# A trunk of two mixer layers on one core: three stage borders, and the second gate stage moved into the attention's filler

## The chip, the cores and the metric

The kernel runs on one core of one Trainium2 chip. Its time is device microseconds of that core for one execution; three executions were timed, and the median counts. One more execution was profiled, and all rows below are from it.

## The reference

All tensors are float32, 1024 tokens by 1024 channels.

```python
def reference(x, p, norm_pre, norm_post, pe_proj, pe_gate, ...):
    h = x
    for i in range(DEPTH):                       # 2 layers
        u = rmsnorm(h, norm_pre[i])
        if i % 2 == 0:
            y = ab_mixer(u, ...)                 # retention and mLSTM heads, @ w_out
        else:
            y = cd_mixer(u, ...)                 # sparse attention and S5 groups, @ w_out
        h = h + rmsnorm(y.astype(h.dtype), norm_post[i])
        h = h + jax.nn.sigmoid(h @ pe_gate[i]) * (p[i] @ pe_proj[i])
    return h
```

`ab_mixer` projects u to the queries, keys, values and gates of 4 retention and 4 mLSTM heads, and multiplies their gated outputs (1024 + 1024 channels) by `w_out`. `cd_mixer` has 16 query heads in 4 groups that attend to compressed, selected and windowed keys (three softmaxes, weighted by gates), and 32 groups of a state-space model with a gated linear unit; 1024 + 512 channels go to its `w_out`. The line with `sigmoid` is what the text calls the gate stage of a layer.

## The kernel before

Every float32 operand of a product is split into a high and a low part (`hi`, `lo`; `split_tile`, `transpose_split`, `load_w`): ScalarE copies the high part, VectorE or POOL subtracts it for the low part, and a product is three matmuls (high by high, low by high, high by low) into one PSUM bank. A 128x1024 by 1024x512 product is thus 24 matmuls of 512 columns. Tokens lie in 8 row tiles of 128; a tile is transposed by TensorE, four 128x128 blocks to a bank (`trp`), before it can be the stationary operand.

The stages in order are: projections and heads of layer 0, each head's results written to DRAM (`mixR` of the retention, `mixM` of the mLSTM); `out_stage(mixR)`, then `out_stage(mixM)`, whose `sink_m` adds the two, normalises (`post_norm`, L894 to L904) and writes `hD[0]`; the gate stage of layer 0 (`gate_stage`), which also prepares the transposed input of layer 1; the projections of layer 1; the sparse attention; the gate stage of layer 1. `in_pairs` runs `front(i)` (load and transpose tile i) ahead of `proj(i, hf)`, the products of a tile's left and right column half.

The whole program is recorded first; a list scheduler then sets each engine's own order by its model of times and by priorities, and each engine executes its list in order, with semaphores between them. SP's list is a DMA queue of its own: a load that waits holds up all loads behind it. A tile pool gives a buffer again when its last reader is done, so a load into a buffer that is still read waits.

The sparse attention is a loop over 32 units, (group, row tile), 8 for each of 4 groups; `group` loads a group's keys and values, `head` a unit's queries and makes its compressed scores, `scores` and `scale` make the probabilities of window and selection, `values` transposes them (`pt`) and multiplies them by the values (`av`). PSUM has there 1 bank for `cs` and `ct`, 2 for scores, 3 for transposes, 1 for `av`, and 1 (`pF`) for the filler. The filler is a generator of other work, which `step` advances by a credit (`share`, so many steps per group): the S5 gated unit, its output product, `p @ pe_proj` (to `ppD`), the output products of the groups, and for the tiles in `LAST[:-NL]`, which are seven of eight, the last output product, the post-norm and the write of `hD[2]`. The post-norm of such a tile (`s` is ScalarE, `v` VectorE, `g` POOL):

```python
for hf in range(2):
    v.tensor_tensor(y[hf], y[hf], product(T, wq[hf], 2), op=OP.add)
    s.activation(ftile(), y[hf], AF.Square, accum_out=ms[:, hf:hf + 1])
...
    s.activation(y[hf], y[hf], AF.Copy, scale=r)
    g.tensor_tensor(y[hf], y[hf], gp, op=OP.mult)
    g.tensor_tensor(y[hf], y[hf], x, op=OP.add)
```

After the attention, all 8 banks go to layer 1's gate stage (`psA`, 3, and `psB`, 5), which reads `hD[2]` tile by tile, and makes the eighth tile (`late_tile`) along the way.

## Time and profile before

| | us |
| --- | --- |
| median of 3 executions | 2372.84 |
| lowest and highest | 2370.55, 2377.94 |
| the profiled execution | 2377.24 |
| its span, first to last instruction | 2375.2 |
| TensorE busy | 2285.4 |
| VectorE, ScalarE, POOL busy | 1467.8, 1069.0, 488.9 |

The span is shorter than the execution's time by what lies ahead of the first and behind the last instruction. Busy times are sums over all stages; which engine is waited for differs from stage to stage. TensorE's mean granted clock over the span is 0.983 of 2.4 GHz.

### The profile page before, as it was taken

Reading aid. Unit: us, or ns where it says so; the run is one execution under the profiler, and the core shown is the slowest. Engines: PE = TensorE matmul, PEld = TensorE weight load, DVE = VectorE, ACT = ScalarE, POOL = GpSimd, SP = SyncE. Lnnn points to the kernel's source line nnn. Section 1 sums busy time; section 2 is a strip of 40 time slices with the busy share of each in tenths; the row PEclk is TensorE's granted clock in tenths of the full one; section 3 lists DMA queues with packets and bytes.
Section 4 is the critical chain, followed back from the end, with each engine's and each line's share of the span. In section 5 each row is a group of like instructions: output and inputs, shape, how many; then the busy total and the mean of one; then the engine's idle time right before and its main releaser. Section 6 shows DMA issues by size and latency. Waiting matters only on the chain.

```text
span 2375.2 us, 34462 instructions
## 1 busy us (share of the span) xinstructions
PE 2285.4 (96%) x11974; PEld 1910.6 (80%) x11974; DVE 1467.8 (62%) x3877; ACT 1069.0 (45%) x2329; POOL 488.9 (21%) x585
## 2 busy tenths in 40 slices
PE   7999999999999999899999999989999989999898
PEld 6888789788887888788888889878888778777677
DVE  6777647755554435344287352368878888888833
ACT  6233323433332332223232232257877777778821
POOL 0122200000000001100000010034445245566610
PEclk9999999999999999999999999989999999999999
...
GB/s 159 91 80 104 101 45 72 27 73 35 63 54 32 261 142 205 125 71 133 113 193 239 142 76 125 95 155 79 106 171 109 124 133 103 139 137 177 145 158 113
DMA packets 264647, 279.26 MB, mean 118 GB/s; under 512 B 54384, under 2 KB 196312, under 8 KB 264442
## 3 DMA queue, kind: packets, MB, share of 16 engines
...
## 4 chain that ended last, share of the span: by engine, by line
PE 85%; DVE 6%; DMA 5%; issue 2%; ACT 1%; SPq 1%; POOL 0%; ACTq 0%; DVEq 0%; POOLq 0%
PE pj L139 41%; PE gp L139 8%; PE op L139 7%; PE fp L139 5%; PE av L139 4%; PE pt L1448 4%; PE sc L139 4%; PE yp L139 2%; PE gl L139 2%; PE trp L214 2%; DVE pr L1424 1%; DVE pthl L1408 1%; DMA q<-aqD 1%; PE pp L139 1%; PE cs L139 1%
## 5 line engine op out<-in xcount | busy, mean ns | idle before, releaser
L139 PE MATMUL pj<-whi,uh 128*128 128x512 f32 (+2 forms) x768 | 277.4, 362 | 4.2 <-ACT whi L163 2.6
L139 PE MATMUL pj<-wlo,uh 128*128 128x512 f32 (+2 forms) x768 | 277.2, 361 | 0.0
L139 PE MATMUL pj<-whi,ul 128*128 128x512 f32 (+2 forms) x768 | 277.0, 361 | 0.0
L1427 ACT ACTIVATE pr<-pr,nm 128x640 f32<-128x640 f32 (+7 forms) x256 | 187.1, 732 | 65.3 <-DVE nm L1424 58.4
L139 PE MATMUL pj<-vh,whi 128*128 128x512 f32 x512 | 204.0, 399 | 0.2 <-ACT vh L218 0.2
L139 PE MATMUL pj<-vh,wlo 128*128 128x512 f32 x512 | 201.9, 394 | 0.0
L139 PE MATMUL pj<-vl,whi 128*128 128x512 f32 x512 | 200.4, 391 | 0.0
L1408 DVE TENSOR_TENSOR pthl<-pt,pthh 128x512 fp32r<-128x512 f32 x264 | 176.6, 682 | 22.0 <-ACT pthh L1407 20.3
L164 DVE SCALAR_TENSOR_TENSOR wlo<-raw,gnp,whi 128x512 fp32r<-128x512 f32 (+3 forms) x248 | 142.4, 610 | 77.2 <-ACT whi L163 76.3
L139 PE MATMUL gp<-whi,mhl 128*128 128x512 f32 x512 | 167.8, 402 | 6.4 <-DVE mhl L219 4.4
L163 ACT ACTIVATE whi<-raw,gnp 128x512 fp32r<-128x512 f32 (+3 forms) x248 | 134.9, 605 | 77.7 <-PE pj L139 34.6
L1448 PE MATMUL pt<-consts,pr 128*128 128x128 f32 x1056 | 164.3, 280 | 5.1 <-DVE pr L1441 1.7
L139 PEld LDWEIGHTS pj<-whi,uh 128*128 128x128 f32 x768 | 144.9, 189 | 27.3 <-ACT whi L163 2.9
L139 PE MATMUL op<-whi,mhl 128*128 128x512 f32 x520 | 165.4, 396 | 0.6 <-ACT mhl L470 0.6
L139 PEld LDWEIGHTS pj<-wlo,uh 128*128 128x128 f32 x768 | 145.2, 189 | 22.6 <-issue 0.7
L139 PEld LDWEIGHTS pj<-whi,ul 128*128 128x128 f32 x768 | 145.0, 189 | 22.2 <-issue 0.2
L1407 ACT ACTIVATE pthh<-pt 128x512 fp32r<-128x512 f32 x264 | 148.7, 591 | 31.0 <-PE pt L1448 22.8
L139 PE MATMUL sc<-kh,q 128*128 128x320 f32 (+5 forms) x384 | 145.5, 381 | 17.3 <-DVE nm L1424 15.8
L1448 PEld LDWEIGHTS pt<-consts,pr 128*128 128x128 f32 x1056 | 132.2, 144 | 31.7 <-DVE pr L1441 2.4
L1441 POOL TENSOR_SCALAR pr<-pr,cf 128x640 f32<-128x640 f32 (+4 forms) x64 | 114.0, 1782 | 98.5 <-DVE cf L1436 49.5
L139 PE MATMUL sc<-kl,q 82*128 82x320 f32 (+5 forms) x384 | 129.9, 340 | 0.0
L139 PEld LDWEIGHTS gp<-whi,mhl 128*128 128x128 f32 x512 | 97.1, 191 | 29.2 <-DVE mhl L219 5.1
...
## 6 DMA issues: line engine op xcount, KB each, us to landing
...
```

The source lines that it names most:

```text
L139: return t.matmul(o, l, r, start=start, stop=stop, **k)
L163: s.activation(hi[:, k], raw[:, k], AF.Copy, scale=gain(kt0 + k))
L164: v.scalar_tensor_tensor(lo[:, k], raw[:, k], gain(kt0 + k), hi[:, k].bitcast(FT), op0=OP.mult, op1=OP.subtract)
L214: t.transpose(ps[:, k * 128:(k + 1) * 128], x[:, (k4 + k) * 128:(k4 + k + 1) * 128], ident)
L1407: s.activation(hi[:dst_shape], ps[:dst_shape], AF.Copy)
L1408: v.tensor_tensor(lo[:dst_shape], ps[:dst_shape], hi[:dst_shape].bitcast(FT), op=OP.subtract)
L1424: v.tensor_tensor_reduce(pr[:, x:y], ps[:, :y - x], mask[:, x:y], op0=OP.add, op1=OP.min, scale=-1.0, scalar=nm[:, 0:1] if c else 3e38, ac ...
L1427: s.activation(pr[:, :nk], pr[:, :nk], AF.Exp, scale=-1.0, bias=nm[:, c:c + 1], accum_out=sums[:, b, h:h + 1])
L1441: (v if eng == "v" else g).tensor_scalar(P[h][:, :nk], P[h][:, :nk], cf[:, h:h + 1], None, op0=OP.mult)
L1448: t.transpose(ps[:, h * 128:(h + 1) * 128], P[h][:, k * 128:(k + 1) * 128], ident)
```

## The change

Border 1: while the mLSTM's last head is finished, the first three row tiles of `mixR` are loaded on SP's queue into buffers that held queries and keys, and that pool stays open until `out_stage(mixR)` ends. Border 2: `out_stage(mixM)` calls `ahead(i)`, which loads row tile 0 of `hD[0]` after it was written, and transposes and splits it before the stage is over; `gate_stage` takes it from `early`. In `proj` the gate's product is issued ahead of that with `pe_proj`. Border 3: `group` loads all keys, then the values; the probabilities of unit 0 are made inside the projections, between their last blocks. The gate stage of layer 1 becomes part of the filler: for all 8 tiles of `LAST`, the filler makes the output product, post-norm, transposes (`ft`, in the filler's one bank), split, and the gate of the left columns (`gated_out(i, 0, ...)`); the split parts go to DRAM (`gT`). Behind the attention, `rest` reads them back and makes the right halves, with the two banks of the scores, in turn with what is left of the filler. The separate stage is removed. `share` has other numbers, `fhi` and `flo` have two buffers, `ppD` is stored times 0.5.

```diff
+            if h == 3 and i in (2, 3, 4):
+                x = first_rows[i - 2] = p2.tile([128, 1024], FT, name="mt", tag="qkq"[i - 2])
+                nc.sync.dma_start(x, mixR[(i - 2) * 128:(i - 1) * 128, :])
...
+            mt = first_rows.pop(i, None)
+            if mt is None:
+                mt = pm_.tile([128, 1024], FT, name="mt", tag="mt")
+                nc.scalar.dma_start(mt[:, :nkt * 128], src[i * 128:(i + 1) * 128, :nkt * 128])
             return split_tile(pw, mt, nkt)
...
+            X = early.get(i)
+            if X is None:
...
+            ps = psA.tile([128, 512], FT, name="gp", tag="psA")
+            proj_tok(ps, local(*T), i, wq[hf], 512)
...
+    early = {}
+    def ahead(i):
+        if i == 4:
+            early[0] = xh_.tile([128, D], FT, name="h1", tag="h1")
+            nc.sync.dma_start(early[0], hD[0][:128, :])
+        if i == 6:
+            hi, lo = (xl_.tile([128, 2, 512], FR, name=n, tag=n).rearrange("p a (b n) -> p (a b) n", n=128)
+                      for n in ("whi", "wlo"))
+            transpose_split(early[0], 0, hi, lo)
+            early[0] = early[0], (hi, lo)
+    out_stage(pr_, mixM, Wo, 8, Ext(dict(a=xa_, b=xb_, l=xl_, m=xm_), "mmllaabb"), gain, sink_m, after=ahead)
...
+            K[b] = kh, kl
+        for b in (1, 0):
+            vt = wsp.tile([128, 2, 512], FR, name="vt", tag=("whi", "wlo")[b]).rearrange("p a (i d) -> p (a i) d", d=128)
             nc.sync.dma_start(vt.bitcast(FT), vD[:, 4 * b + gg].rearrange("(i p) a d -> p i (a d)", p=128))
-            K[b] = kh, kl, vt
...
+        def probabilities(K, hd, u, b, sums):
+            gg, i = u
+            P = scores(K[b], hd[0], hd[1], i, b, hd[3], sums)
+            scale(P[0], P[2], b, sums, gate_of(gg, i))
+            return P
+        hs_, first = {}, {}
+        for n, _ in enumerate(gen):
+            if n in (2, 7):
+                hs_[len(hs_)] = head(*units[len(hs_)])
+            if n == 10:
+                KV = {0: group(0)}
+            if n in (12, 13):
+                if not first:
+                    sums0 = nh.tile([128, 2, 4], FT, name="sums", tag="sums")
+                first[13 - n] = probabilities(KV[0], hs_[0], units[0], 13 - n, sums0)
...
-            wq = wlast[0] = [[load_w(W2, [(hf * 512, 512)], 6, 2)] for hf in range(2)]
-            for i in LAST[:-NL]:
+            wq = [[load_w(W2, [(hf * 512, 512)], 6, 2)] for hf in range(2)]
+            gw[0] = [load_w(Wg, [(0, 512)], 2 * k, 2, wp=xf) for k in range(4)]
+            gw[1] = [load_w(Wg, [(512, 512)], 0, 2)]
+            for i in LAST:
...
-                    nc.sync.dma_start(hD[2][rows, hv[hf]], y[hf])
+                nc.sync.dma_start(hD[2][rows, hv[1]], y[1])
                 yield
-        wlast = [None]
+                hi, lo = (pf.tile([128, 4, 256], FR, name=n, tag=n, bufs=2).rearrange("p a (b k) -> p (a b) k", k=128)
+                          for n in ("fhi", "flo"))
+                for hf in range(2):
+                    ps = pF.tile([128, 512], FT, name="ft", tag="pf")
+                    for k in range(4):
+                        t.transpose(ps[:, k * 128:(k + 1) * 128], y[hf][:, k * 128:(k + 1) * 128], ident)
+                    p3_, ks = ps.rearrange("p (k n) -> p k n", k=4), slice(4 * hf, 4 * hf + 4)
+                    s.activation(hi[:, ks], p3_, AF.Copy)
+                    v.tensor_tensor(lo[:, ks], p3_, hi[:, ks].bitcast(FT), op=OP.subtract)
+                    yield
+                if i != LAST[-1]:
+                    for a, x in enumerate((hi, lo)):
+                        nc.sync.dma_start(gT[i, :, a, :], x.bitcast(FT).rearrange("p k n -> p (k n)"))
+                yield from gated_out(i, 0, (hi, lo), y[0], pF, "pf")
+                if i == LAST[-1]:
+                    yield from gated_out(i, 1, (hi, lo), y[1], pF, "pf")
+        def gated_out(i, hf, T, h, pool_, tag):
+            rows, hs = slice(i * 128, (i + 1) * 128), slice(hf * 512, (hf + 1) * 512)
+            ps = pool_.tile([128, 512], FT, name="gp", tag=tag)
+            for k in range(0, 8, 4):
+                proj_tok(ps, local(*(x[:, k:k + 4] for x in T)), 0, gw[hf][k // 2:], 512, nkt=4, start=k == 0, stop=k == 4)
+                yield
+            pp = pf.tile([128, 512], FT, name="pp", tag="fin", bufs=4)
+            nc.sync.dma_start(pp, ppD[rows, hs])
+            th = pf.tile([128, 512], FT, name="th", tag="fo", bufs=4)
+            s.activation(th, ps, AF.Tanh, scale=0.5)
+            v.scalar_tensor_tensor(th, th, 1.0, pp, op0=OP.add, op1=OP.mult)
+            (v if done else g).tensor_tensor(th, th, h, op=OP.add)
+            nc.sync.dma_start(dst_[rows, hs], th)
...
+        def rest():
+            def fetch(i):
+                T = [np_.tile([128, 1024], FR, name="g" + x, tag="pr0", bufs=5).rearrange("p (k n) -> p k n", k=8) for x in "hl"]
+                h = np_.tile([128, 640], FT, name="gr", tag="pr1", bufs=4)[:, :512]
+                for a in range(2):
+                    nc.sync.dma_start(T[a].rearrange("p k n -> p (k n)").bitcast(FT), gT[i, :, a, :])
+                nc.sync.dma_start(h, hD[2][i * 128:(i + 1) * 128, 512:])
+                return T, h
+            X = {0: fetch(LAST[0])}
+            for n, i in enumerate(LAST[:-1]):
+                if n + 1 < len(LAST) - 1:
+                    X[n + 1] = fetch(LAST[n + 1])
+                T, h = X.pop(n)
+                yield from gated_out(i, 1, T, h, pS, "sc")
...
-        share = {0: 30, 1: 26, 2: 20, 3: 64}
+        credit = [0.0]
+        share = {0: 24, 1: 34, 2: 22, 3: 50}
...
+        gw[1] += [load_w(Wg, [(512, 512)], 2 * k, 2) for k in range(1, 4)]
+        done.append(True)
+        gens = [fill, fill, rest()]
+        while gens:
+            for x in list(gens):
+                if x in gens and next(x, gens) is gens:
+                    gens = [y for y in gens if y is not x]
...
-    qx_ = ExitStack()
-    psB = qx_.enter_context(tc.tile_pool(name="psB2", bufs=5, space=PSUM, reuse_waits="tile"))
-    psA = qx_.enter_context(tc.tile_pool(name="psA2", bufs=3, space=PSUM, reuse_waits="tile"))
...
-        def late_tile(i, y):
...
-        gate_stage(pw, 1, ext1, hD[2], out if out is not None else dbg["o"], ppD=ppD, order=[7, 6, 5, 0, 1, 2, 4, 3],
-                   late={i: late_tile for i in LAST[-NL:]})
```

The first place is the second border, where the last output matmuls of layer 0 are followed by the first gate products. VectorE's rows of before (`y1` are the output rows under post-norm, `mhl` is the pair of high and low parts, `trp` the bank of the transposes):

```order
L224 TENSOR_SCALAR rsa_9000<-ms_8998 128x1 [waits Activation_49]
L902 SCALAR_TENSOR_TENSOR y1_8940<-y1_8940,rsb_9002,gpost_8317 128x1024 [waits Pool_49]
L903 TENSOR_TENSOR y1_8940<-y1_8940,xr_9004 128x1024 [waits DMAHW2_49,DVE_49]
L1006 TENSOR_TENSOR y1_8968<-y1_8968,op_9009 128x512 [waits PE_49]
L224 TENSOR_SCALAR rsa_9038<-ms_9036 128x1 [waits Activation_49]
L902 SCALAR_TENSOR_TENSOR y1_8968<-y1_8968,rsb_9040,gpost_8317 128x1024 [waits Pool_49]
L903 TENSOR_TENSOR y1_8968<-y1_8968,xr_9042 128x1024 [waits DMAHW5_49,DVE_49]
L219 TENSOR_TENSOR mhl_9112<-trp_9113,mhl_9112 128x512 [waits Activation_49]
L219 TENSOR_TENSOR mhl_9112<-trp_9120,mhl_9112 128x512 [waits Activation_49]
L936 TENSOR_TENSOR pT_9132<-ptp_9129,pT_9132 128x256 [waits DMAHW5_49,Activation_49]
```

and of the change, where tile 0's parts are called `whi` and `wlo`, since they lie in weight buffers:

```order
L1016 TENSOR_TENSOR y1_8942<-y1_8942,op_8973 128x512 [waits PE_49]
L219 TENSOR_TENSOR wlo_9012<-trp_9020,whi_9011 128x512 [waits Activation_49]
L224 TENSOR_SCALAR rsa_9002<-ms_9000 128x1 [waits Activation_49]
L909 SCALAR_TENSOR_TENSOR y1_8942<-y1_8942,rsb_9004,gpost_8317 128x1024 [waits Pool_49]
L910 TENSOR_TENSOR y1_8942<-y1_8942,xr_9006 128x1024 [waits DMAHW1_49,DVE_49]
L1016 TENSOR_TENSOR y1_8970<-y1_8970,op_9027 128x512 [waits PE_49]
L224 TENSOR_SCALAR rsa_9056<-ms_9054 128x1 [waits Activation_49]
L909 SCALAR_TENSOR_TENSOR y1_8970<-y1_8970,rsb_9058,gpost_8317 128x1024 [waits Pool_49]
L910 TENSOR_TENSOR y1_8970<-y1_8970,xr_9060 128x1024 [waits DMAHW4_49,DVE_49]
L945 TENSOR_TENSOR pT_9133<-ptp_9130,pT_9133 128x256 [waits Activation_49]
L219 TENSOR_TENSOR mhl_9138<-trp_9139,mhl_9138 128x512 [waits Activation_49]
L219 TENSOR_TENSOR mhl_9138<-trp_9146,mhl_9138 128x512 [waits Activation_49]
```

Tile 0's second low part (`wlo_9012<-trp_9020`) has moved ahead of the last two post-norms (L909, L910); the low parts of tile 1 (`mhl_9138`) stand where tile 0's stood.

The second place is the border from the projections to the sparse attention. SP's rows of before (`vt` is a group's value tile, `kh` and `kl` its keys, `q2` and `q3` a unit's queries, `zt` a projection's result on its way to DRAM):

```order
L1113 DMA zD_92<-zt_13660 128x512 [waits DMAHW2_49,DVE_49]
L1113 DMA zD_92<-zt_13705 128x512 [waits DMAHW3_49,DVE_49]
L1128 DMA vt_13674<-vD_88 128x8x128 [waits DMAHW4_49,PE_49]
L1126 DMA kl_13673<-kD_87 64x1024 [waits DMAHW5_49,PE_49]
L1127 DMA kl_13673<-akD_89 18x1024 [waits DMAHW6_49]
L1113 DMA zD_92<-zt_13734 128x512 [waits DMAHW7_49,DVE_49]
L1124 DMA kh_14753<-kD_87 64x1024 [waits DMAHW0_49,PE_49]
L1125 DMA kh_14753<-kD_87 64x1024 [waits DMAHW1_49]
```

and of the change:

```order
L1136 DMA zD_92<-zt_13709 128x512 [waits DMAHW4_49,DVE_49]
L1136 DMA zD_92<-zt_13790 128x512 [waits DMAHW5_49,DVE_49]
L1353 DMA q2_14150<-qD_86 128x4x128 [waits DMAHW6_49,PE_49]
L1354 DMA q3_14151<-qD_86 64x4x128 [waits DMAHW7_49,PE_49]
L1355 DMA q3_14151<-aqD_91 18x4x128 [waits DMAHW0_49]
L1153 DMA vt_13653<-vD_88 128x8x128 [waits DMAHW1_49,PE_49]
L1153 DMA vt_13651<-vD_88 128x8x128 [waits DMAHW2_49,PE_49]
L1146 DMA kh_14585<-kD_87 64x1024 [waits DMAHW3_49,PE_49]
L1147 DMA kh_14585<-kD_87 64x1024 [waits DMAHW4_49]
```

All keys of group 0 are loaded earlier; the queries of unit 2 and then both value tiles stand behind the last projection results, and each value tile still waits for TensorE.

The third place is the end of the program. TensorE's rows of before, in the separate gate stage (`h1` is a tile of rows, `gp` the bank of a product):

```order
L139 MATMUL gp_23963<-whi_23490,mhl_23691 128x512 x2
L139 MATMUL gp_23963<-wlo_23491,mhl_23691 128x512
L214 MATMUL trp_23885<-consts_75,h1_23849 128x128 [waits DVE_49,PE_49]
L214 MATMUL trp_23885<-consts_75,h1_23849 128x128 x3
L214 MATMUL trp_23892<-consts_75,h1_23849 128x128 [waits PE_49]
L214 MATMUL trp_23892<-consts_75,h1_23849 128x128 x3
L139 MATMUL gp_23963<-whi_23490,mhl_23691 128x512
L139 MATMUL gp_23995<-whi_23472,mhl_23834 128x512 [waits Activation_49]
L139 MATMUL gp_23995<-wlo_23473,mhl_23834 128x512
L139 MATMUL gp_23995<-whi_23472,mhl_23834 128x512 x2
```

and of the change (`fp` is the bank of an output product, `ft` that of the transposes, `fy` the row halves after the post-norm; tile 1 of the last four):

```order
L139 MATMUL fp_23397<-whi_21652,fhi_23341 128x512 [waits Activation_49]
...
L139 MATMUL fp_23397<-whi_21652,flo_23342 128x512 [waits Pool_49]
...
L139 MATMUL fp_23407<-whi_21658,fhi_23341 128x512 [waits DVE_49]
...
L1613 MATMUL ft_23496<-consts_75,fy_23337 128x128 [waits DVE_49,Pool_49]
L1613 MATMUL ft_23496<-consts_75,fy_23337 128x128 x3
L1613 MATMUL ft_23558<-consts_75,fy_23338 128x128 [waits DVE_49,Pool_49]
L1613 MATMUL ft_23558<-consts_75,fy_23338 128x128 x3
L139 MATMUL gp_23567<-whi_21664,fhi_23494 128x512 [waits DVE_49]
```

Before, the next tile's transposes stand among the products of another; now a tile's output products, transposes and gate products follow one another. The transposes wait for POOL, whose rows for that tile are:

```order
L226 TENSOR_TENSOR rsb_23477<-rsa_23475,mhalf_79 128x1 [waits DVE_49]
L1604 TENSOR_TENSOR fy_23337<-fy_23337,fin_23479 128x512 [waits DMAHW3_49,Activation_49]
L1604 TENSOR_TENSOR fy_23338<-fy_23338,fin_23486 128x512 [waits DMAHW2_49,PE_49,DMAHW5_49,Activation_49,Pool_49]
L1605 TENSOR_TENSOR fy_23337<-fy_23337,fin_23480 128x512 [waits DMAHW4_49,Pool_49]
L1605 TENSOR_TENSOR fy_23338<-fy_23338,fin_23487 128x512 [waits DMAHW6_49,Pool_49]
L1497 TENSOR_TENSOR flo_23629<-zn_22725,fhi_23628 128x2x128 [waits PE_49,Activation_49]
L226 TENSOR_TENSOR rsb_23693<-rsa_23691,mhalf_79 128x1 [waits DVE_49]
```

These are the power of the norm (L226), the two halves times the gain (L1604), the residual added to them (L1605), the low part of the next tile's input (L1497), and the next tile's power.

## Rows read from the trace of the kernel before

**Rows 1.** The page, part 1: busy time, share of the span, instructions.

```profile
PE 2285.4 (96%) x11974; PEld 1910.6 (80%) x11974; DVE 1467.8 (62%) x3877; ACT 1069.0 (45%) x2329; POOL 488.9 (21%) x585
```

**Rows 2.** The page, part 4: the chain that ended last, by engine.

```profile
PE 85%; DVE 6%; DMA 5%; issue 2%; ACT 1%; SPq 1%; POOL 0%; ACTq 0%; DVEq 0%; POOLq 0%
```

**Rows 3.** Windows: stretch, length, busy us (instructions) per engine, clock, DMA share, GB/s.

```profile
960.00:1000.00 40.00, 33.56 (x148) 26.96 (x148) 16.34 (x21) 8.52 (x16) 5.35 (x4) 0.87 0.37 120
...
1545.00:1592.00 47.00, 40.25 (x187) 32.29 (x187) 28.33 (x84) 26.06 (x46) 19.45 (x14) 0.78 0.72 182
...
2035.00:2160.00 125.00, 116.28 (x645) 96.60 (x643) 106.49 (x281) 98.02 (x185) 76.92 (x65) 0.99 0.48 148
...
2160.00:2262.00 102.00, 89.52 (x449) 68.24 (x447) 87.55 (x267) 83.44 (x206) 68.13 (x68) 0.93 0.53 169
```

**Rows 4.** Windows: the half-clock stretches behind the second border and the attention.

```profile
970.40:980.60 10.20, 5.79 (x13) 4.11 (x14) 5.73 (x4) 1.40 (x2) 2.78 (x2) 0.50 0.54 177
...
2264.00:2270.80 6.80, 4.44 (x19) 3.91 (x19) 3.75 (x5) 1.66 (x3) 3.56 (x2) 0.50 0.82 278
```

**Rows 5.** The chain in order of time, last stage: start, us, what.

```profile
2346.07 0.87 PE trp L214 x8
...
2346.95 22.44 PE gp L139 x96
...
2370.77 0.69 DVE h L956
```

**Rows 6.** The same view at the first border.

```profile
769.89 3.60 DMA mt<-mixR
```

**Rows 7.** Timeline at the first border, ScalarE: start, us, engine, line, instruction.

```profile
770.77 1.93 ACT L163 ACTIVATE whi<-raw,cols 128x512 fp32r<-128x512 f32 x3
```

**Rows 8.** Timeline at the second border (idle time before, and its releaser, in brackets).

```profile
966.68 1.23 DVE L903 TENSOR_TENSOR y<-y,xr 128x1024 f32<-128x1024 f32 x1
...
970.42 0.80 PE L139 MATMUL gp<-whi,mhl 128*128 128x512 f32 x1 [2.06 <-ACT mhl L218]
...
971.88 2.41 POOL L160 TENSOR_TENSOR wlo<-raw,whi 128x1024 fp32r<-128x1024 f32 x1 [1.11 <-ACT whi L159]
...
972.12 3.25 DVE L903 TENSOR_TENSOR y<-y,xr 128x1024 f32<-128x1024 f32 x1
...
976.03 1.22 PE L139 MATMUL gp<-whi,mhl 128*128 128x512 f32 x2 [4.38 <-DVE mhl L219]
```

**Rows 9.** The chain in order of time at the third border.

```profile
1545.47 4.77 DMA vt<-vD
...
1550.33 8.80 DMA vt<-vD
...
1559.14 8.38 DMA fin<-y5D
```

**Rows 10.** Groups by line, attention: xcount | busy, mean ns | idle before, releaser.

```profile
L1555 DVE TENSOR_TENSOR fy<-fy,fp 128x512 f32<-128x512 f32 x14 | 9.5, 680 | 3.5 <-issue 2.9 <-PE fp L139 0.4
...
L1556 ACT ACTIVATE fin<-fy 128x512 f32<-128x512 f32 x14 | 8.8, 626 | 5.1 <-DVE fy L1555 4.2 <-issue 0.5 <-POOL fy L1566 0.4
...
L1564 ACT ACTIVATE fy<-fy,rsb 128x512 f32<-128x512 f32 x14 | 9.3, 718 | 1.1 <-POOL rsb L226 1.1
...
L1565 POOL TENSOR_TENSOR fy<-fy,fin 128x512 f32<-128x512 f32 x14 | 17.8, 1286 | 8.0 <-ACT fy L1564 4.9 <-DMA fin<-in_norm_post_dram 2.5 <-ACT pthh L1407 0.6
...
L1566 POOL TENSOR_TENSOR fy<-fy,fin 128x512 f32<-128x512 f32 x14 | 19.0, 1368 | 0.0
```

**Rows 11.** The same view before the attention, POOL: the power of the norms.

```profile
L226 POOL TENSOR_TENSOR rsb<-rsa,mhalf 128x1 f32<-128x1 f32 x24 | 13.4, 559 | 335.2 <-DVE rsa L224 335.2
```

**Rows 12.** Timeline after the attention, TensorE.

```profile
2266.36 1.97 PE L214 MATMUL trp<-consts,h 128*128 128x128 f32 x8 [4.55 <-DMA h<-hD]
```

**Rows 13.** Groups by line, last stage: the two halves of a split.

```profile
L219 DVE TENSOR_TENSOR mhl<-trp,mhl 128x512 fp32r<-128x512 f32 x16 | 10.8, 686 | 10.1 <-ACT mhl L218 9.9
...
L218 ACT ACTIVATE mhl<-trp 128x512 fp32r<-128x512 f32 x16 | 9.0, 596 | 14.4 <-PE trp L214 14.1
```

135 lines of the change are left out of this document (53 added, 82 removed).

## The prediction

> **What bounds the kernel now.** I read the page first: TensorE is busy for 2285 of the 2375 us [rows 1], and the chain that ended last is TensorE for 85% and waits on VectorE and DMA for most of the rest [rows 2]. So an edit is worth what it takes from TensorE's idle time, from its stretches at half clock, or from the last matmul's tail. Next I cut the span into stages [rows 3] to see where TensorE stands still: in the steady stages it is full, and what is lost lies at the borders and in the sparse attention. The window 960:1000 has it busy 33.56 of 40 us at clock 0.87, 1545:1592 40.25 of 47 at 0.78, 2160:2262 89.52 of 102 at 0.93. In [rows 4] the reader sees what follows a stall: right behind it the granted clock stands at 0.50, which is 1.2 of 2.4 GHz, for 10.2 us at the second border and for 6.8 us after the attention. Half clock over 6.8 us costs at most 3.4 us.
>
> The unit of the sums is the steady interval of a 128x512 matmul: 96 in 22.44 us, 0.234 us each, and 8 transposes in 0.87 us, 0.109 each [rows 5]. All sums are made against the profiled execution (2377.24 us, span 2375.2), which is 4.4 us above the median of the runs, 2372.84; I apply the difference to the median. A change of less than 0.3% (7.1 us) can't be told from none here.
>
> **Border 1 (mLSTM to the first output stage).** Before, the first row tile is requested when the last gate product is read, and lands after 3.60 us [rows 6]. The change has three row tiles loaded earlier on SP's queue, so the 20 transposes of five half tiles (2.2 us) follow at once. The wait for the DMA goes (3.8 us with its hops). What is late next: the first split, since ScalarE still has four weight conversions ahead of it, three of which took 1.93 us [rows 7]; the 2.2 us of transposes cover most of them. I take 3 us; ends 2.4 (the DMA wait less one uncovered pair of conversions) and 5.5 (the wait and half of the low clock behind it).
>
> **Border 2 (second output stage to the gate).** The first product waits 4.38 us for VectorE's low part [rows 8]. VectorE was in the last tiles' post-norms, and one of these took 3.25 us instead of the 1.23 of its neighbour while POOL's weight split of 2.41 us ran. The order rows in the section on the change show that tile 0's split now stands ahead of these post-norms: 24 products (5.6 us) can then follow the last output matmul with nothing missing, and tile 1's split has these 5.6 us plus its own transposes as cover. Without this cover it would wait as before. Removed: 2.06 and 4.38 us of stall and the half clock behind them. Window 960:1000 is short by 40 - 33.56 = 6.4 us of busy time, and the 5.79 us of work in the 10.2 us at half clock would take 2.9. I take 8.5; ends 6 (POOL's split still holds something up) and 9.4.
>
> **Border 3 (projections to sparse attention).** The chain there is three DMA in a row: 4.77 and 8.80 us for the two value tiles, of which the first was issued only when the last projection was under way, then 8.38 us for a filler input behind them in SP's queue [rows 9]. The change makes the probabilities of unit 0 between the last two blocks of 24 projection matmuls (2 x 5.6 us of cover for VectorE's maxima and ScalarE's exponentials), loads all keys first, and keeps the two value loads where they were: they still wait for the last projection to release its weight buffers, and now stand behind three query loads. So the scores' pacing by VectorE is covered, the wait for the value tiles is not: the first value product needs a tile that lands 4.8 to 8.8 us after its release, with 18 projection matmuls (4.2 us), a few scores and 16 probability transposes (1.7 us) as cover. Window 1545:1592 holds 6.75 us without TensorE and 0.22 x 47 = 10.3 us of missing clock, 17 in all. I take 7; ends 4 and 14.
>
> **Sparse attention.** The filler now takes the gate of tiles 7, 6 and part of 5 there. Counted from the order, TensorE's work behind the last value product falls from 99.6 us (384 products, 64 transposes, 12 of the output) to 88.1 us (310 products, 48 of the output, 40 transposes), so 11.5 us more work must fit into the attention. It is hidden by idle time: 2035:2160 and 2160:2262 have 8.7 and 12.5 us of it. The other engines get no more: three post-norms leave (one before, four now lie behind the last unit), each 4 POOL operations of 1.29 us and one of 0.56, ScalarE 2.7, VectorE 1.4 [rows 10, 11]; three halves of a product and three tiles' splits come in. I take +2 us; ends -17 (all the idle time and the clock missing from the last window, 21.2 + 0.07 x 102 = 28, less 11.5) and +5.
>
> **The tail.** This is the large term. Before, it is one dense run: 4.55 us until the tile h arrives [rows 12], then 99.6 us of work, 3.4 us of half clock, 5.8 us from the last matmul to the end (2369.4 to 2375.2) [rows 5]: 113.4 us, as the trace has it (2261.8 to 2375.2). After, four of eight tiles still have their output product, post-norm, transposes and gate to do, one tile behind the other through one PSUM bank. Walked by TensorE's order:
> - 46 right-half products, 10.8.
> - Tile 0: 4 transposes, ScalarE 0.60, VectorE 0.69 [rows 13], and again the same, since the second four need the same bank: 3.5, with hops between engines 4.2. Then 24 products, 5.6.
> - Tile 1: bank released by the tanh, 1.0; 6 products 1.4; VectorE 0.68 and a hop, 0.9; 6 products 1.4; then nothing to do until the post-norm is through: VectorE 0.68, ScalarE 0.63, POOL 0.56, ScalarE 0.71, three POOL operations of 1.29, 6.5 in all; with the reading of ScalarE's sum, two one-column VectorE operations, hops and the matmul's drain I put 7.9. Splits 4.2, products 5.6. Sum 22.4.
> - Tiles 2, 3, 4: the 0.9 is replaced by 19 right-half products (4.4), sum 25.9 each. Behind the second 6 products stand 5, 29 and 29 right-half products (1.2, 6.8, 6.8 us), so the 7.9 stays the length of the path.
> - Release 1.0, the last 24 products 5.6, end 5.8.
>
> Sum 133.1 us, of which 39 is TensorE waiting. Gaps of up to 6.7 us are longer than the 4.55 us behind which [rows 4] show half clock; for two such stretches I add 6, ends 0 and 14 (one in each of four tiles). Tail 139, 25.6 more than before; ends 20 and 36 (clock low in all, and 2 us for the halves that go through DRAM and back).
>
> The page "Perfetto Trace Analysis" of the Trainium skill, section "Matmuls", wants independent matmul groups to rotate through different PSUM banks, so that one is emptied during the next. It speaks against this tail, which leaves eight banks for one; by it alone, each tile would lose the two bank waits (1.0 + 2.5 us) that the walk has, 17 us of the 25.6. The trace of before agrees: with its several banks the 8 transposes of a tile take 0.87 us with products right behind [rows 5].
>
> **Sum.** -3 - 8.5 - 7 + 2 + 25.6 = +9.1: 2386.3 for an execution like the profiled one, 2381.9 on the scale of the median. I forecast **2382 us**, slightly slower: what the borders give, the uncovered chains of the tail take back.
>
> **Rivals.**
> - *The attention takes up the work for nothing and more* (faster). POOL is busy 68.13 and ScalarE 83.44 of the last 102 us, and the last quarter loses three post-norms. If that frees TensorE's idle time and clock there, the end -17 instead of +2 applies: 2382 - 19 = 2363. It decides where the last value product comes at 2229 or earlier (my walk has 2245). Against it: VectorE, 87.55 of 102 busy, isn't relieved. Chance 0.22.
> - *The borders pay for the tail* (same): upper ends at all three, 5.5 + 9.4 + 14 = 28.9 against 25.6 + 2: 2371.5. For it: all of 17 us at border 3 is idle or slow. Against: the value loads still wait. Chance 0.26.
> - *Half clock in every tile of the tail* (slower, 14 instead of 6): 2390. For it: TensorE is busy 9.5 of tile 1's 22.4 us. Chance 0.12.
> - *POOL's four operations held up by VectorE.* [rows 8] show the two in each other's way (3.25 for 1.23 us), and in three tiles two VectorE operations of 0.69 us with both inputs in SBUF fall into POOL's chain: 1.4 us per tile, 4 in all: 2386. Chance 0.06. The page "SBUF — State Buffer" of the Trainium skill, section "SBUF: two separate sides", has the port pair of the two as an exclusive lock for the whole instruction; the 3.25 us agree.
> - The forecast, 2380 to 2386: 0.34. Faster 0.22, same (2365.7 to 2380) 0.26, slower 0.52.
>
> The range reaches down to the first rival's upper reach, 2358 (that with border 1 and 3 a little above my values), and up to 2400 (all lower border values, 6 less, and a tail at +36).
>
> **What the profile will show.** Right: no DMA wait of TensorE at border 1; 24 products directly behind the last output matmul at border 2; 16 score pairs ahead of the last projection block; in the tail four gaps of 6 to 8 us (tile 1, 2) or 1 to 2 us (3, 4) in which the transposes wait for POOL, and pairs of waits of about 1.3 us for VectorE at the split; last value product near 2245, tail near 139. Wrong: a tail under 128, or a last value product away from 2245 by over 10 us.

## The result and the profile after

The changed kernel has a median of 2417.02 us (four executions, 2415.25 to 2421.62) beside 2374.69 for the kernel before on the same chip: a ratio of 1.0168 [1.0148, 1.0189], so some 40 us slower. A second measurement of the same kernel gave 1.015 [1.0134, 1.0166]. The forecast was 2382 us, its range 2358 to 2400; the time lies above it. The profiled execution took 2421.62 us, its span is 2419.8; it is the slowest of the four, and the later profile of the same kernel has a span of 2415.3.

The page of the changed kernel, parts 1 and 4, beside [rows 1, 2]:

```profile
PE 2301.0 (95%) x11974; PEld 1918.7 (79%) x11974; DVE 1463.2 (60%) x3871; ACT 1072.0 (44%) x2333; POOL 496.9 (21%) x594
...
PE 80%; DVE 7%; issue 5%; DMA 5%; ACT 2%; POOL 1%; SPq 1%; DVEq 0%; ACTq 0%; POOLq 0%
```

TensorE has as many instructions as before, and is the chain's engine for 80% in place of 85%: time was added in which it waits or is slowed. Where, the windows say (columns as in [rows 3]):

```profile
700.00:780.00 80.00, 77.62 (x433) 66.01 (x433) 39.20 (x130) 26.63 (x74) 4.46 (x8) 1.00 0.18 60
960.00:1000.00 40.00, 39.34 (x189) 32.48 (x188) 17.50 (x24) 11.40 (x20) 7.23 (x5) 1.00 0.37 126
2035.00:2160.00 125.00, 115.84 (x607) 93.56 (x606) 105.95 (x275) 94.90 (x181) 74.96 (x64) 0.95 0.50 155
2160.00:2262.00 102.00, 93.32 (x499) 75.63 (x498) 81.84 (x259) 75.01 (x184) 47.38 (x50) 0.95 0.39 128
2267.00:2420.00 153.00, 106.22 (x399) 79.69 (x399) 35.80 (x55) 28.59 (x56) 31.52 (x29) 0.85 0.53 179
```

The second border is full now: 39.34 of 40 us busy at clock 1.00, where it had 33.56 at 0.87. The last window is the tail, from the last value product (2266.9) to the end: 153 us, in which TensorE is busy for 106 only. Before, the last value product came at 2261.3 and the tail took 113.9. The tail is 39 us longer, and that is nearly the whole slowdown: what lies ahead of it ends 5.6 us later here, and 1.0 us earlier in the second profile of the same kernel (2260.3, tail 155.0). Of the distance to the forecast it is about half: the prediction had the last value product near 2245 and a tail of 139, so 15 to 22 us were missed ahead of the tail and 14 to 16 in it.

**The two borders of layer 0.** The chain in order of time at border 1, where [rows 6] have a DMA of 3.60 us:

```profile
770.99 0.48 ACT whi L163
...
771.54 1.94 ACT whi L163 x3
773.47 0.48 ACT mhl L218
...
774.23 0.98 ACT mhl L218 x2
...
775.25 0.73 PE op L139 x2
```

The DMA is gone, and ScalarE's weight conversions ahead of the first split are late next, as the prediction said. At border 2 the timeline of TensorE from 962 to 985 has one wait in place of the 2.06 and 4.38 us of [rows 8]:

```profile
972.74 0.66 PE L214 MATMUL trp<-consts,h 128*128 128x128 f32 x4 [0.66 <-DVE pT L945]
```

The last product of the first output stage starts at 868.20 us (before 871.79), the last gate product of layer 0 at 1087.25 (before 1101.18): 3.6 us gained at border 1, and 13.9 with border 2.

**The third border.** TensorE's timeline, the last scores of the early probabilities and the first value products:

```profile
1548.52 0.41 PE L139 MATMUL sc<-kh,q 128*128 128x320 f32 x1 [0.31 <-DVE zt L1135]
...
1552.33 0.49 PE L139 MATMUL av<-pthh,vt 128*128 128x512 f32 x1 [3.25 <-ACT pthh L1475]
1558.17 0.80 PE L139 MATMUL av<-pthl,vt 128*128 128x512 f32 x1 [5.35 <-DVE pthl L1476]
```

TensorE stands for 3.25 and 5.35 us, and not for a value tile: it waits for the parts of the transposed probabilities (`pthh`, `pthl`). ScalarE makes the high part behind a step of the next unit's selection of keys, for which it waits 1.79 us. VectorE's timeline shows why the low part is late, and a row of SP's queue when the write that it waits for was issued:

```profile
1547.78 0.69 DVE L1135 SCALAR_TENSOR_TENSOR zt<-zt,pj 128x512 f32<-128x512 f32 x1 [1.51 <-ACT zt L1134]
...
1549.15 2.18 DVE L1369 TENSOR_TENSOR scc<-scc,m 128x192 f32<-128x192 f32 x1
...
1557.42 1.88 DVE L1476 TENSOR_TENSOR pthl<-pt,pthh 128x512 fp32r<-128x512 f32 x3 [1.65 <-DMA zD<-zt]
```

```profile
1550.36 0.35 SPq L1136 DMA_DIRECT2D zD<-zt  x1
```

Up to 1555.8 it works through the next unit's selection of keys (L1367 to L1392), which stands ahead in its order, and then the low part waits for a write: the last projection result, made at 1547.78, has still to leave through SP's queue before its memory can hold the probabilities' parts. That write was issued at 1550.36, behind both value tiles (1543.0) and most of the next group's keys; the section on the change has the value tiles behind the last projection results, which holds for all of these but the last.

**The tail.** TensorE's timeline from the gate of tile 0 to that of tile 1:

```profile
2286.44 0.52 PE L139 MATMUL gp<-whi,fhi 128*128 128x512 f32 x1 [1.41 <-DVE flo L1616]
...
2294.49 0.50 PE L139 MATMUL fp<-whi,fhi 128*128 128x512 f32 x1 [0.69 <-ACT th L1635]
...
2296.93 0.50 PE L139 MATMUL fp<-whi,fhi 128*128 128x512 f32 x1 [0.78 <-DVE fy L1594]
...
2305.72 1.12 PE L1613 MATMUL ft<-consts,fy 128*128 128x128 f32 x4 [7.13 <-POOL fy L1605]
2308.34 1.08 PE L1613 MATMUL ft<-consts,fy 128*128 128x128 f32 x4 [1.50 <-DVE flo L1616]
2310.84 0.79 PE L139 MATMUL gp<-whi,fhi 128*128 128x512 f32 x1 [1.41 <-DVE flo L1616]
2311.43 0.63 PE L139 MATMUL gp<-wlo,fhi 128*128 128x512 f32 x1
...
2314.28 0.40 PE L139 MATMUL gp<-whi,flo 128*128 128x512 f32 x1
...
2334.20 1.12 PE L1613 MATMUL ft<-consts,fy 128*128 128x128 f32 x4 [5.96 <-POOL fy L1605]
2337.39 1.09 PE L1613 MATMUL ft<-consts,fy 128*128 128x128 f32 x4 [2.08 <-DVE flo L1616]
```

Every wait of the walk is there: the bank behind the tanh, VectorE's sum, 7.13 us for POOL (predicted 7.9), the two split halves. What the walk had too small stands in the same rows: behind the long wait the products take 0.63 us instead of 0.40, until 2314. The last two rows are of tile 2, where the second wait is 2.08 us instead of 1.50; tiles 3 and 4 have 3.03 and 2.54 there. VectorE's row ahead of the low part, and POOL's at that time, show what made it late:

```profile
2334.31 1.60 DVE L1636 SCALAR_TENSOR_TENSOR th<-th,pp 128x512 f32<-128x512 f32 x1 [5.33 <-DMA pp<-ppD]
```

```profile
2332.88 2.49 POOL L1605 TENSOR_TENSOR fy<-fy,fin 128x512 f32<-128x512 f32 x2
```

An operation of VectorE with two inputs in SBUF, which takes 0.69 us alone, ran beside POOL's and took 1.60; in tiles 3 and 4 it took 1.60 and 1.70. The window of one such stretch, and the groups of TensorE's waits over the tail (busy, mean ns | idle before and its releasers):

```profile
2303.90:2314.10 10.20, 5.46 (x16) 4.02 (x17) 1.38 (x2) 1.50 (x3) 3.72 (x4) 0.50 0.45 162
```

```profile
L139 PE MATMUL gp<-whi,fhi 128*128 128x512 f32 x48 | 23.7, 495 | 7.7 <-DVE flo L1616 7.1 <-ACT th L1635 0.7
L139 PE MATMUL gp<-whi,gl 128*128 128x512 f32 x56 | 23.1, 412 | 2.7 <-DMA gl<-gT 2.7
...
L1604 POOL TENSOR_TENSOR fy<-fy,fin 128x512 f32<-128x512 f32 x10 | 12.6, 1276 | 11.3 <-issue 8.0 <-ACT fy L1603 3.3
L1605 POOL TENSOR_TENSOR fy<-fy,fin 128x512 f32<-128x512 f32 x10 | 12.6, 1271 | 0.2
...
L1613 PE MATMUL ft<-consts,fy 128*128 128x128 f32 x40 | 8.2, 341 | 24.6 <-POOL fy L1605 14.0 <-DVE flo L1616 10.7
```

The transposes alone wait for 24.6 us. A mean clock of 0.85 over 153 us is 0.15 x 153 / 0.5 = 46 us at half clock, in seven stretches; six follow a wait, the seventh lies behind the last matmul and costs nothing. In the stretch shown TensorE works for about half of it (5.46 of 10.20); 46 us so filled lose about 46 x 0.53 / 2 = 12 us, where the prediction allowed 6. A count in the trace agrees: 73 matmuls start at half clock, where a product of 512 columns takes 0.43 us to the next one instead of 0.23, and lose 12 to 13 us.

### The profile page after: what moved, and what is told of

The parts are those of the page before. It is cut to its first block, busy times and chain, and to the rows that moved or that the text cites. A ratio compares the mean times of both kernels' runs of the same rounds, so it can differ in the third digit from the quotient of the medians.

```text
span 2419.8 us, 34583 instructions
## 1 busy us (share of the span) xinstructions
PE 2301.0 (95%) x11974; PEld 1918.7 (79%) x11974; DVE 1463.2 (60%) x3871; ACT 1072.0 (44%) x2333; POOL 496.9 (21%) x594
## 4 chain that ended last, share of the span: by engine, by line
PE 80%; DVE 7%; issue 5%; DMA 5%; ACT 2%; POOL 1%; SPq 1%; DVEq 0%; ACTq 0%; POOLq 0%
PE pj L139 41%; PE op L139 7%; PE gp L139 5%; PE fp L139 5%; PE sc L139 4%; PE av L139 4%; PE pt L1484 3%; PE yp L139 2%; DVE pr L1425 2%; PE gl L139 1%; DVE pthl L1476 1%; PE trp L214 1%; PE cs L139 1%; PE pp L139 1%; PE hp L139 1%
## 5 line engine op out<-in xcount | busy, mean ns | idle before, releaser
L139 PE MATMUL av<-pthl,vt 128*128 128x512 f32 x264 | 116.8, 443 | 10.1 <-DVE pthl L1476 9.8
L139 PE MATMUL av<-pthh,vt 128*128 128x512 f32 x264 | 111.1, 421 | 5.7 <-ACT pthh L1475 5.5
```

The lines of the kernel that those rows point to most:

```text
L139: return t.matmul(o, l, r, start=start, stop=stop, **k)
```

## The experiments

All ratios are against the kernel before on the same chip. "Tail" is from the last value product to the end in the profiled execution; "group 0 to 3" are the stretches of the attention between the ends of the groups' last units.

**The parts apart.** The three borders without the gate in the filler, borders 1 and 2 alone, the gate alone, and the gate with borders 1 and 2:

```diff
 # a_borders: the change, without the gate in the filler
-                yield from gated_out(i, 0, (hi, lo), y[0], pF, "pf")
...
-        gens = [fill, fill, rest()]
...
+    gate_stage(pw, 1, ext1, hD[2], ...)
 # c_borders12: a_borders, without border 3
-                first[13 - n] = probabilities(KV[0], hs_[0], units[0], 13 - n, sums0)
...
 # b_gate_only: the kernel before, with the gate in the filler
+                yield from gated_out(i, 0, (hi, lo), y[0], pF, "pf")
...
+        gens = [fill, fill, rest()]
 # m_gate_borders12: b_gate_only, with borders 1 and 2
+                x = first_rows[i - 2] = p2.tile([128, 1024], FT, name="mt", tag="qkq"[i - 2])
...
+    out_stage(pr_, mixM, ..., after=ahead)
```

> All three border edits, gate stage of layer 1 left as a stage of its own as before. Theory 1 (the attention pays for what the filler gained, the borders are innocent): groups 1 to 3 take 528 us as before, tail 113, so the gain of 15 us seen at the end of group 0 remains: about 2360. Theory 2 (the early probabilities and the keys-first loads of border 3 disturb the attention): groups 1 to 3 longer by 8 us or more, 2368 or above.

Measured: 0.9981 [0.997, 0.9991]; tail 117.7. Groups 1 to 3 took 524.4 us, no longer than before, as theory 1 had it; but the time is theory 2's, since group 0 ends only 9 us earlier than before (17 in c_borders12) and the tail is 4 us longer.

> Borders 1 and 2 alone. By the trace of the change they gave 4.3 and 8.7 us of TensorE's time; if nothing behind them moves, 2362. If border 3 added something, the kernel with all three is faster than this one by 2 to 4 us; the prediction's own figures were 2363 here and 7 more for border 3.

Measured: 0.993 [0.9915, 0.9946]; tail 117.3. Borders 1 and 2 give 16.6 us, and border 3 takes back 12 of them.

> The gate stage in the filler alone, borders as before. Theory 1 (the filler's edit costs it all): groups 1 to 3 near 548 us, tail near 152, 2430 to 2435. Theory 2 (border 3's edits share the loss in the attention): groups 1 to 3 near 535, about 2420.

Measured: 1.0137 [1.0113, 1.0161]; tail 155.2, last value product at 2252.6. Groups 1 to 3 took 513.7 us, less than either theory had; it is the tail that costs.

> The gate stage in the filler and borders 1 and 2, border 3 as before. If the parts add up: 16 us for borders 1 and 2, minus 35 for the gate: 2394 on the first chip, ratio 1.007. If the gate's attention time depends on the order that the scheduler finds, it lies apart from that by up to 10 us.

Measured: 1.0113 [1.0096, 1.013]; tail 151.5: the parts don't add up (1.007). So the gate costs 32 us on the kernel before, 43 beside borders 1 and 2 (1.0113 - 0.993), 44 in the whole change (1.0168 - 0.9981). In the profiles the tails differ by 41, 34 and 35 us; ahead of the tail the gate costs -8.7, +6.6 and +17.2 (+10.6 by the second profile of the change). So most of it is the tail. And border 3 costs 13 us beside the gate too (1.0168 - 1.0113), or 9 by the second measurement.

**The tail: one cause or several.** The prediction's walk has one chain per tile: bank, post-norm on POOL, split. Each link was shortened by itself.

```diff
 # e_dve_norm
-                    g.tensor_tensor(y[hf], y[hf], gp, op=OP.mult)
-                    g.tensor_tensor(y[hf], y[hf], x, op=OP.add)
+                    (v if done else g).tensor_tensor(y[hf], y[hf], gp, op=OP.mult)
+                    (v if done else g).tensor_tensor(y[hf], y[hf], x, op=OP.add)
 # d_banks: transposes and left gate products of the tail in the attention's three banks
+        def bank(name):
+            return pT.tile([128, 512], FT, name=name, tag="pt") if done else pF.tile([128, 512], FT, name=name, tag="pf")
 # f_dummies: after the post-norms of tiles 1 and 2, into an unused bank
+                        for _ in range(22):
+                            mm(dm, z[:, :128], z, True, True)
```

> The change, with the last two steps of the post-norm of tiles 2 to 4 of the tail (times gain, plus residual) on VectorE instead of POOL; every engine's order in the attention and TensorE's order in the tail stay. If POOL's chain is what the tail waits for: three steps of 0.69 instead of 1.29 us, 1.8 us less in tile 2, and in tiles 3 and 4 the remaining wait of 0.6 us and 1 to 1.5 us of the wait between the two transposes gone: 6 us less, 2411. If the bank or the clock decides, 2 us or less.

Measured: 1.0113 [1.0095, 1.0132]; tail 148.5, 4.5 us less. (One order of the tail took 153.0 and 155.0 us in two executions, so these differences are good to about 2 us.)

> The change, with the tail's transposes and left products in the three banks of the attention's transposes instead of the filler's one; the attention is the same. If the one bank costs what the trace shows (five waits of 0.84 us for the tanh, five of 1.6 us for the split before the products, and of the five waits between the two transposes 1.6 us each): 15 to 18 us less, about 2400. If POOL's chain only takes their place, 5 us or less.

Measured: 1.0118 [1.0101, 1.0135]; tail 144.9, 8.1 less. The eight transposes of tile 2 now follow each other, but still wait for POOL, and new waits stand behind them (timeline of TensorE, tail):

```profile
2332.95 2.34 PE L1616 MATMUL ft<-consts,fy 128*128 128x128 f32 x8 [5.97 <-POOL fy L1608]
2346.57 0.53 PE L139 MATMUL fp<-whi,fhi 128*128 128x512 f32 x1 [3.71 <-DVE fy L1597]
...
2376.22 0.79 PE L139 MATMUL fp<-whi,fhi 128*128 128x512 f32 x1 [7.22 <-DVE fy L1597]
```

> Both edits of the tail together. If the tail's waits are all from bank and POOL: 22 to 26 us less than the change, about 2393, and the tail still above the 113 us of before, since tile 1's chain stays. If half clock follows the last value product anyway, less than 15.

Both edits together measured 1.0117 [1.0101, 1.0133], tail 143.7, 9.3 less: hardly more than the banks alone. The link that is shortened gives its time to the next one. What that link is, TensorE's longest wait in this tail and VectorE's row for the sum that it waits for show:

```profile
2375.30 0.79 PE L139 MATMUL fp<-whi,fhi 128*128 128x512 f32 x1 [9.50 <-DVE fy L1597]
```

```profile
2374.56 0.69 DVE L1597 TENSOR_TENSOR fy<-fy,fp 128x512 f32<-128x512 f32 x1 [6.67 <-DMA fy<-yD]
```

It is a load: the rows of the next tile (`yD`), to which the output product is added, have not arrived.

> The change, with 22 matmuls (5.1 us) whose results nobody reads, in the gaps of 7.1 and 6.1 us of the tail's tiles 1 and 2; one ScalarE copy per tile added. If half clock there follows from the gaps: the 10.2 and 13.6 us at half clock go, 5 to 7 us less, 2411. If half clock comes from elsewhere, or the extra copy delays the chain as much, 2417 to 2419.

Measured: 1.0147 [1.0132, 1.0162], tail 151.3. This kernel adds 22 matmuls of 512 columns, whose results nobody reads, in each of the two longest gaps, so that TensorE doesn't stand still there. Its tail window:

```profile
2264.00:2415.00 151.00, 114.63 (x443) 86.56 (x442) 34.42 (x55) 29.53 (x58) 31.95 (x29) 0.90 0.56 186
```

Half clock falls from 46 us to 0.10 x 151 / 0.5 = 30, and the tail only by 1.7. Most of the half clock that went had held waiting, not work: the kernel's own matmuls at half clock fall from 73 to 58, by the count in the traces 1.9 us, and that is what the tail gained. The waits of 1.5 and 1.4 us for the two split halves, which are still there, again have half clock behind them. So this run doesn't tell clock and chain apart; it shows that half clock costs by the matmuls that run in it, 11 to 13 us here, the smaller part of the 39. To test the chain, its order was changed: the next tile's output product and post-norm are issued ahead of this tile's transposes.

```diff
 # p_pipelined: on de_banks_dve, front = product and post-norm, back = transposes, split, gate
+                y = yield from front(i)
+                if held:
+                    yield from back(*held)
+                    held = None
+                if done and i != LAST[-1]:
+                    held = i, y
+                else:
+                    yield from back(i, y)
...
-            th = pf.tile([128, 512], FT, name="th", tag="fo", bufs=4)
+            if done:
+                th = np_.tile([128, 640], FT, name="th", tag="pr1", bufs=4)[:, :512]
```

> The change with both edits of the tail, and in the tail the output product and post-norm of the next tile recorded ahead of the transposes of the one before. If the tail's length is that of chains which have nothing beside them: only tiles 0 and 1 still run in turn, tail 120 to 125 us, 28 us less than the change, about 2390. If half clock or the DMA of the row halves bounds it, 138 or more.

Measured: 1.0048 [1.0033, 1.0063]. The window of its tail, and the longest wait that is left (tile 1, whose place the edit doesn't change), then tile 2's:

```profile
2258.50:2383.80 125.30, 97.34 (x399) 74.80 (x399) 41.01 (x67) 28.46 (x56) 16.46 (x17) 0.92 0.66 224
```

```profile
2297.46 1.12 PE L1617 MATMUL ft<-consts,fy 128*128 128x128 f32 x4 [6.96 <-POOL fy L1606]
...
2325.67 0.66 PE L1617 MATMUL ft<-consts,fy 128*128 128x128 f32 x4 [0.70 <-DVE fy L1606]
```

Tail 125.5 for the same 399 matmuls, 18 us less than de_banks_dve and 28 less than the change, and the wait of 5.96 us that tile 2 has in the change became 0.70. The waits of 3.7 and 9.5 us behind the loads are gone as well: with the product, its loads stand earlier in SP's queue, and the edit also gives the tail's results (`th`) other buffers. Which of the three gave how much was not tried apart. Half clock goes too (0.08 x 125.3 / 0.5 = 20 us, 34 matmuls), about 5 of the 18 us.

**The filler's numbers.** The change also altered `share`. The old numbers of groups 0 to 2 in the new kernel, numbers between, and such numbers in the kernel before:

```diff
-        share = {0: 24, 1: 34, 2: 22, 3: 50}
+        share = {0: 30, 1: 26, 2: 20, 3: 50}   # h_old_shares
+        share = {0: 26, 1: 32, 2: 22, 3: 50}   # n1_shares_after
-        share = {0: 30, 1: 26, 2: 20, 3: 64}
+        share = {0: 28, 1: 28, 2: 20, 3: 64}   # n2_shares_before
```

> The change, with the filler's credits of groups 0 to 2 as before (30, 26, 20). If the new credits cause the low clock in groups 1 and 2, these fall from 182 and 195 us back to 177 and 186, and the time to about 2405, less what group 0 takes more. If the added gate work or the double buffers cause it, the sum of groups 0 to 3 stays within 4 us, 2417.

> The change with two filler steps moved from group 1 to group 0 (26, 32 for 24, 34): the same work, a new order in the attention. If the filler's load decides the time of the attention, groups 1 to 3 stay within 3 us of the change's 548. If the order that the scheduler finds decides, they move by 5 us or more in either direction.

> The kernel before with two filler steps moved from group 0 to group 1 (28, 28 for 30, 26): the same work, a new order in the attention. If the load decides, 2374 and groups 1 to 3 within 3 us of 528; if the order decides, 5 us or more away in either direction.

Measured: 1.0195 [1.0173, 1.0216], 1.0174 [1.0146, 1.0202] and 1.0012 [0.9999, 1.0024]. None of these numbers gives the time back. They move it: with the old numbers groups 1 and 2 do fall (171 and 179 us) and the last value product comes at 2254.7, but then the tail holds more work and takes 163.0. Groups 1 to 3 took 536.6 us in n1_shares_after and 530.8 in n2_shares_before (before 527.6). The first is 11.5 below the change's 548.1, but only 2.0 below those of its second profile (538.6, next run), so it decides nothing.

> The change itself once more, beside the next three on one chip, with a second profile. The order of every engine is the one already traced, so the tail should be 153 us within 2; the attention, if its time at one order differs between executions as d_banks, e_dve_norm and f_dummies let it seem, may end up to 8 us earlier than in the first trace.

The change once more: 1.015 [1.0134, 1.0166], last value product at 2260.3, where the first profile had 2266.9, in the same order of instructions. The tail is 155.0, groups 1 to 3 take 538.6 us instead of 548.1. So the attention alone scatters by 6 to 10 us from execution to execution, and what one profile shows there must not be explained below that.

**The third border.** First the memory of the last two projection results, whose late write holds up the low parts; then all keys first without early probabilities; last the early loads without the early probabilities.

```diff
 # j_own_zt: on a_borders
+                    if c and half and m > 1:
+                        zt = zl[0].tile([128, 512], FT, name="zt", tag="zl")
 # k_keys_first: on c_borders12
-            K[b] = kh, kl, vt
+            K[b] = kh, kl
+        for b in (1, 0):
+            vt = wsp.tile([128, 2, 512], FR, name="vt", tag=("whi", "wlo")[b])...
 # s_late_probs: on a_borders
-                first[13 - n] = probabilities(KV[0], hs_[0], units[0], 13 - n, sums0)
...
-            if n == 0:
-                Pw, Ps = first[1], first[0]
-            else:
...
                 step(gg, nw / 2)
```

> All three border edits as in a_borders, with the last two projection results in a buffer pool of their own, so that the memory of the transposed probabilities' parts is not that of a tile still on its way to DRAM. If that write is what the first value products wait for (3.4 and 5.6 us at border 3): 6 us faster than a_borders, ratio to before near 0.9955. If the value tiles or something else is late next: as a_borders, 0.998.

Measured: 0.9948 [0.9928, 0.9968], 8 us better than a_borders (3 by the spans, 2364.2 and 2367.4): the write of the last results was a real wait. The scheduler's order changed with it, though: VectorE now makes the low parts between the steps of the selection, so the gain belongs to both. And the wait that the prediction had named is the next one (timeline of TensorE, the first value product):

```profile
1553.70 0.76 PE L139 MATMUL av<-pthh,vt 128*128 128x512 f32 x1 [2.67 <-DMA vt<-vD]
```

> Borders 1 and 2, and of border 3 only the order of the loads (all keys of a group, then its values); no early probabilities. If the loads' order is what border 3 lost beyond the write of the last projection results (4 us): ratio 0.995. If the early probabilities did: 0.993, as with borders 1 and 2 alone.

Measured: 0.9895 [0.9878, 0.9911], 8 us better than c_borders12 and the best of all. That is more than either forecast: the order of the loads was a gain, not a part of the loss.

> All three borders without the filler's gate, but the probabilities of unit 0 made in unit 0 again, while the queries and all keys are still loaded as early as the change loads them. Before this, the three borders together measured 0.9981 and borders 1 and 2 with keys loaded first 0.9895; in between lies about 20 us. If the probabilities between the projection blocks are what costs (VectorE then serves two users in its one order): 0.988 to 0.992. If it is the loads that are brought forward (their place in the DMA queue, ahead of the last results): 0.996 to 1.000. Half of each: near 0.994.

Measured: 0.9897 [0.9873, 0.9922], as good as k_keys_first. So the loads brought forward cost nothing, and the early probabilities cost 20 us by the ratios (13 by the spans, 2367.4 and 2354.6). Where they go, two windows and TensorE's groups by line (1505 to 1586) show, of a_borders and then of s_late_probs:

```profile
1550.00:1586.00 36.00, 26.23 (x157) 21.77 (x156) 24.58 (x63) 21.33 (x41) 17.31 (x14) 0.86 0.69 189
1505.00:1586.00 81.00, 68.95 (x339) 54.30 (x338) 42.59 (x110) 37.38 (x67) 22.88 (x16) 0.92 0.43 121
```

```profile
L139 PE MATMUL sc<-kh,q 128*128 128x320 f32 (+2 forms) x30 | 12.3, 410 | 3.3 <-DVE nm L1425 2.7 <-DVE zt L1135 0.3
...
L139 PE MATMUL gl<-fhi,whi 128*128 128x256 f32 x16 | 4.7, 292 | 0.0
```

```profile
1550.00:1586.00 36.00, 34.27 (x229) 31.47 (x230) 28.22 (x79) 26.23 (x50) 17.25 (x15) 0.91 0.37 112
1505.00:1586.00 81.00, 72.93 (x398) 60.95 (x397) 41.77 (x117) 38.62 (x71) 23.88 (x18) 0.96 0.46 129
```

```profile
L139 PE MATMUL sc<-kh,q 128*128 128x320 f32 (+2 forms) x33 | 13.6, 412 | 1.8 <-DVE nm L1425 1.3
...
L139 PE MATMUL gl<-fhi,whi 128*128 128x256 f32 x32 | 9.2, 288 | 0.0
```

At about 1586 the first unit is through in both. With its scores made early, TensorE is busy for 26 of the last 36 us, without for 34; over the 81 us 59 matmuls more have run without, 48 of them the filler's `gl` (three such groups, x32 for x16). In the changed loop unit 0 calls no `step`, since its scores, beside which the filler advances, are gone. Its value products then wait for ScalarE, VectorE and the write with nothing beside them, and the early scores are paced by VectorE too (2.7 us of waits, 1.3 when made in unit 0). What was moved forward was no gain; the filler paid for it, and by the end of group 0 a_borders is 7.3 us behind (1729.7 and 1722.4). Counted from 1505 on, TensorE has then waited 19.1 us and 11.3, of which 11.6 and 7.4 fall before the end of the first unit; and the filler is still 22 products of 512 columns behind. That the missing `step` is the reason was read from the code and these rows, not tried by itself, and it accounts for the first unit only. The rest of the 13 us lies in group 1 (4.9) and the tail (3.6), less about 3 in groups 2 and 3; its way there, and the 7 us between spans and ratios, stay open.

**Can the gate pay at all?** The pipelined tail with borders 1 and 2, and the same with keys first:

```diff
 # q_gate_best: m_gate_borders12 with front and back of p_pipelined
 # r_gate_keys_first: q_gate_best with
-            K[b] = kh, kl, vt
+            K[b] = kh, kl
```

> The gate stage in the filler with the pipelined tail of p_pipelined, borders 1 and 2, border 3 as before. If the filler's own price is the tail alone: the 27 us of m_gate_borders12 over before less 28, ratio 1.000; still above borders 1 and 2 alone (0.993), because the tail stays above 113 us. If the attention pays besides, 1.005.

Measured: 0.9957 [0.9942, 0.9971], better than both forecasts, but still 6 us above c_borders12.

> Borders 1 and 2, keys loaded first, the gate in the filler and the tail in which the next tile's output product stands ahead of this tile's transposes. If the parts add, 0.9957 less the 0.0035 that keys first gave without the filler: 0.992, still above the 0.9895 without the filler. If the filler's work and the earlier keys use the same idle time of the sparse attention: 0.995 to 0.997.

Measured: 1.0 [0.9984, 1.0017]. Keys first cost 10 us here, where they gave 8 without the gate; neither forecast had that. Both tails are 125.5; the loss is in groups 0 and 1 (6 and 5 us), and its cause stays open. The tail of k_keys_first for comparison:

```profile
2237.00:2352.00 115.00, 103.51 (x461) 83.69 (x461) 39.98 (x59) 21.10 (x38) 5.23 (x4) 0.97 0.36 128
```

It holds 62 matmuls more than the pipelined tail and is 10 us shorter.

## Why the prediction was wrong

The sum was -3 - 8.5 - 7 + 2 + 25.6 = +9.1. By ratios and profiles, it should have read -16.6 for borders 1 and 2, +12 for border 3, about +5 for the attention (the remainder) and +39 for the tail: +40. Two steps failed, one with its sign: the gain at border 3, and the size of the tail.

- **Border 1 and 2 (-11.5, measured -16.6).** Right in mechanism, with the waits that were named. At the last gate product of layer 0 the change is 13.9 us ahead of before, and c_borders12 14.9; the rest lies in the attention, which the same edits reorder (groups 1 to 3: 523.0 for 527.6 us), and is within its scatter.
- **Border 3 (-7, ends -4 and -14, measured +12).** The failed step is "the first value product needs a tile that lands 4.8 to 8.8 us after its release": it named the wrong wait, and held the rest for cover. In the change TensorE waited 3.25 and 5.35 us for the transposed parts. These were late because VectorE's one order has the next unit's selection ahead of them, and because their memory belonged to a result that had not been written out (8 us by j_own_zt, together with the order that came with it). The value tile stood right behind: without that write it is what the first value product waits for, 2.67 us. "The scores' pacing by VectorE is covered" failed too: the early scores wait for it as well, and the filler that had stood in such gaps had no step. Making the scores late again gave more than the 12 us back (s_late_probs).
- **The attention (+2, ends -17 and +5).** The rival that it takes up the work for nothing fits b_gate_only: the last value product comes 8.7 us earlier than before, with 11.5 us more work ahead of it, in one execution of each. In the change the rival's mark (2229) was missed by over 30 us. With the borders the same work costs 6.6 to 17 us ahead of the tail, with another order of the attention each time; why there and not alone was not settled.
- **The tail (139, +25.6, ends 20 and 36; measured 153.0 and 155.0, +39).** The walk named every wait but the first; most of its terms were sized too small. From row to row against the walk: the start 4.6 us, tile 0 1.4, tile 1 1.9, tiles 2 to 4 4.0, 4.3 and 2.7, the end 0.9: 19.8 over 133.1, of which 6 had been allowed for. The step that failed is "for two such stretches I add 6": six stretches at half clock came, also behind waits of 2.7 and 3.0 us, and cost 12 to 13 us, near the upper end of 14. That was the third rival (2390). What it lacks is the fetch of `gT` at the start (2.72 us, which the walk left out) and the second wait for the split in tiles 2 to 4, 2.08, 3.03 and 2.54 us where tiles 0 and 1 have 1.50. POOL's waits were not too small: 7.13 and 5.96 us, 0.7 below the walk's.
- **POOL held up by VectorE.** The two did meet, but it was VectorE that was held up. POOL's ten L1604 and ten L1605 take 1.276 and 1.271 us, no more than before [rows 10]; VectorE's L1636 takes 1.60, 1.60 and 1.70 us in tiles 2 to 4 instead of 0.69, and the low part stands behind it in VectorE's order. The late low parts cost 3.2 us in all, near the 4 of the rival.
- **The rule on banks.** The Trainium skill, "Perfetto Trace Analysis", section "Matmuls", wants independent matmul groups to rotate through different PSUM banks. By the walk's bank waits that would have been worth 17 us; d_banks took 8.1 off the tail. The rule points the right way; about half of its price had other waits standing behind it, for POOL and for the loads of the next tile's rows.

The larger mistake is of the whole: a stage that was dense (99.6 us of work in 113.9) gave up 11.5 us of work and lost the independent tiles that filled its waits. In the traces TensorE's waits in the tail grow from 5.2 us to 40.1. The chance of slower, 0.52, was on the right side, in part by luck: the forecast had 16.5 us of gain ahead of the tail, of which nothing was left. The range was too low because every border in it was a gain, and because the tail's waits were added at their shortest, in a chain where every delay adds up.

The fastest version of all, ahead of both kernels, is k_keys_first: both borders of layer 0 and the keys first, 0.9895 [0.9878, 0.9911]; s_late_probs is as fast.
